# Expert gates of tokens 128 to 255 by scattered writes in HBM, those of tokens 0 to 127 by one-hots laid out per token

## The chip, the cores and the metric

The kernel runs on one core of a Trainium2 chip. The metric is the time of one execution on the device, from the first to the last instruction, in microseconds (us); a kernel's time is the median of its timed runs. The engines are TensorE (PE in the rows, PEld for its weight loads), VectorE (DVE), ScalarE (ACT), GpSimd (POOL) and SyncE (SP), each of which works through its own instruction stream in order and waits for others by semaphores.

## The reference

x is [1, 256, 1024] f32. Two transformer blocks run one after the other. The first has mixed attention and retention and a gated FFN (w_gate, w_up, w_down); the second has a gated mixing and a banded attention, and then the part that the change touches: a layer of 16,384 experts of which each token uses 8 heads times 16.

```python
def block(xb):                                    # 128 tokens, twice
    q = (xb @ w_query).reshape(128, 8, 2, 128)
    sc = einsum('thpd,hpkd->thpk', q, sub_keys)   # 128 keys in each half
    s_top, i_top = top_k(sc, 16)
    cand = s_top[:, :, 0, :, None] + s_top[:, :, 1, None, :]
    cand_idx = i_top[:, :, 0, :, None] * 128 + i_top[:, :, 1, None, :]
    best, pos = top_k(cand, 16)                   # of the 256 sums
    eidx = take_along_axis(cand_idx, pos)         # the expert: a * 128 + b
    g = softmax(best)
    h = gelu(einsum('thkd,td->thk', expert_u[eidx], xb))
    return einsum('thk,thkd->td', g * h, expert_v[eidx])
```

## The kernel before

The experts are not gathered. `peer` (L702) computes the hidden value of all 16,384 experts for all 256 tokens, and multiplies it by a matrix of gates that is zero wherever a token did not choose an expert. S, [128, 128, 256] f32, holds it: the first index of an expert, a, on the partitions, the second, b (called j), in the middle, and the token last.

Every f32 weight is taken in two parts. `unit_` (L80) loads 128x1024 f32 (`raw`, L89, on SyncE's DMA queue), ACT rounds it to `whi` (L94) and DVE subtracts to get `wlo` (L95). `mm3` (L105) then makes three matmuls, lines L107, L108 and L109.

The stages that matter here, in order of time:

- The first block's FFN: 22 steps f, each with a unit of w_gate and one of w_up.
- Queries and selection. `query(c)` makes the 16 halves of the queries and their scores. `choose` (L729) finds the top 16 of each head with DVE's MAX8 instructions, and when all eight heads are done, `decode` (L745) turns the positions into a, b and the softmax gate. These steps form a list, and `pump` takes a budget of them at a time between the matmul groups (PQ and PU), so that DVE's work lies beside PE's.
- First layer, `first_layer(j)` for j = 0 to 127: 24 matmuls of 256 columns from a unit of `peer_u`, then the gelu for every pair of j (L933 for tokens that already have their gate in S, with DVE's multiply L934; L936 for the others).
- Combine. From the point at which the decode is done, `combine` (L851) makes the gate matrix for four tokens at a time, beside the first layer. A one-hot row of a, A, and a one-hot row of b times the gate, G (two f16 parts, so that the gate keeps its precision), are multiplied on PE, summed over the 128 choices: 8 matmuls of 128 columns (L872), and DVE and ACT put the result into S (L875, L878). 64 combines make 512 such matmuls. They stand in pairs, in runs of 16 between the first layer's matmuls. A and G are laid out [128, 128, 4], with the four tokens innermost, so the 128 columns of one token lie four elements apart:

```python
nc.tensor.matmul(C[:, t * 128:t * 128 + 128], lhsT=A[:, :, t], rhs=G[i][:, :, t], start=i == 0, stop=i == 1)
```

- Second layer, for j = 0 to 127: S[:, j] is split in two parts (`split`, ACT L151 and DVE L152, tiles `keys` and `q`), and 12 matmuls of 512 columns (L974) multiply it by a unit of `peer_v`. The residual x3, parked in HBM, is loaded again behind j = 32 (L991), added at the end, and the result stored.

The program is ordered by a scheduler that follows the order of the code, except that `unit_` runs at a higher priority, so that loads and conversions of weights stand well ahead of their use.

Of the kernel before, what the change touches and what calls it, by code (L numbers as in the profile page):

```python
# [7 lines left out]
F32 = mybir.dt.float32  # L8
# [14 lines left out]
GP = 115  # L23
# [5 lines left out]
T = 256  # L29
D = 1024  # L30
# [5 lines left out]
for _n, _w in (("norm_mix", 8), ("norm_ffn", 8), ("final_norm", 8), ("ln_mix", 8), ("ln_ffn", 8),  # L36
               ("ret_gain", 8), ("gmlp_gain", 4), ("q_g", 1), ("k_g", 1), ("sinks", 8)):
    SMALL[_n] = (_o, _o + _w)
    _o += _w
# [3 lines left out]
class Net:  # L43
# [36 lines left out]
    def unit_(self, src, n, pieces, engine, between):  # L80
# [11 lines left out]
        for i in range(pieces):  # L92
            s = slice(i * n // pieces, (i + 1) * n // pieces)
            self.last_copy = nc.scalar.activation(hi[:, s], raw[:, s], AF.Copy).ins  # L94
            (engine or nc.vector).tensor_tensor(out=lo[:, s], in0=raw[:, s], in1=hi[:, s].bitcast(F32),  # L95
                                                op=OP.subtract)
# [17 lines left out]
    def gemm_t(self, ps, src, hl, K, k0=0, first=True, last=True, parts=None, engine=None):  # L114
        """ps[n, t] += W[k, n] x[k, t] for one unit of up to 8 k."""
# [12 lines left out]
    def gemm_t_late(self, jobs, hl):  # L128
        """gemm_t of several (ps, src), with the last k after all others."""
# [6 lines left out]
    def gemm_n(self, src, hl):  # L136
        """two banks, one per 128 tokens, of [t, 512] for a chunk of 512 columns."""
# [19 lines left out]
    def rsqrt(self, y, ss, n, scale, pool=None):  # L157
        """y = (ss * scale + eps)^-1/2, all [128, n]."""
# [22 lines left out]
    def token_sums(self, acc):  # L181
        """[128 t, 2] from [128 d, 256 t] summed over d."""
# [6 lines left out]
    def rows(self, r, name):  # L189
        """[128, 256] with r of token t in column t, in every partition."""  # L190
# [40 lines left out]
    def block1(self, actp):  # L231
        nc, a, tc = self.nc, self.a, self.tc
        mult, add, sub = OP.mult, OP.add, OP.subtract
        with ExitStack():
# [16 lines left out]
            self.iota16 = self.const.tile([128, 128, 4], F16, name="iota16")  # L251
            nc.sync.dma_start(out=self.iota16, in_=a["iota16"])
# [107 lines left out]
            with ExitStack() as s1:  # L360
                p = self.pool("ffn", 1, s1)
                p2 = self.pool("ffn2", 2, s1)
                hid = self.new_acts(p, KF, "hid", 1)
                early = []
                for f in range(KF):
# [336 lines left out]
    def peer(self, st, x3, h, acc):  # L702
        nc, a, tc = self.nc, self.a, self.tc
        mult, add, sub = OP.mult, OP.add, OP.subtract
        with tc.using_default_side("right"):
            xb = self.new_acts(self.pool("xb", 1), tag="xb", bufs=1)
            gs = self.pool("gs", 1).tile([128, 4, T], F16, name="gs")
            qp = self.pool("query", 1)
            late = ExitStack()
            p = self.pool("topk", 1, late)  # L710
        hand = self.pool("hand", 2, st)
        x3t = tc.dram_tile([2, 128, D], F32, name="x3t")
        stop = p.tile([128, 8, 2, 2, 16], F32, name="stop")
        itop = p.tile([128, 8, 2, 2, 16], U32, name="itop")
        best = p.tile([128, 8, 2, 16], F32, name="best")
        pos = p.tile([128, 8, 2, 16], U32, name="pos")
# [12 lines left out]
        def choose(hd):  # L729
            sc = scores.pop(hd)  # L730
            yield from top16([(sc[:, tb, e], stop[:, hd, tb, e], itop[:, hd, tb, e])
                              for tb in range(2) for e in range(2)], 205)
            cand = p.tile([128, 2, 80], F32, name="cand", bufs=2)
            s1, s2 = stop[:, hd, :, 0], stop[:, hd, :, 1]
# [10 lines left out]
        def decode():  # L745
            e16 = p.tile([128, 2, 16, 8], F16, tag="cand", name="e16", bufs=2)
            t8 = p.tile([128, 8, 2, 16], U32, tag="sc", name="t8", bufs=SC)
            dec = p.tile([128, 4, 2, 16, 8], F16, tag="stop", name="dec")
            a16, b16 = dec[:, 0], dec[:, 1]

            def spot(x):
                return x.rearrange("p t k h -> p h t k")

            for e in range(2):
                yield 340, lambda: nc.vector.tensor_copy(spot(dec[:, 2 + e]), itop[:, :, :, e])
            yield 340, lambda: nc.vector.tensor_scalar(t8, pos, 56, None, op0=add)
            yield 340, lambda: nc.vector.tensor_scalar(spot(e16), pos, 72.0, 0.0, op0=sub, op1=OP.max)
            yield 340, lambda: nc.vector.tensor_scalar(t8, t8, 3, None, op0=OP.logical_shift_right)
            yield 340, lambda: nc.vector.tensor_scalar(spot(a16), t8, 8.0, 0.0, op0=sub, op1=OP.max)
            yield 340, lambda: nc.vector.tensor_scalar(t8, pos, 16.0, 8.0, op0=OP.is_lt, op1=mult)  # L760
            yield 340, lambda: nc.vector.scalar_tensor_tensor(spot(b16), spot(a16), -8.0, pos, op0=mult, op1=add)
            yield 340, lambda: nc.vector.scalar_tensor_tensor(spot(b16), t8, -8.0, spot(b16), op0=add, op1=add)
            yield 200, lambda: nc.vector.tensor_tensor(out=a16, in0=a16, in1=e16, op=add)
            yield 200, lambda: nc.vector.tensor_tensor(out=b16, in0=b16, in1=e16, op=sub)
            ex = p.tile([128, 8, 2, 16], F32, tag="itop", name="ex")
            yield 340, lambda: nc.vector.tensor_tensor(out=ex, in0=best,
                                                       in1=best[:, :, :, 0:1].to_broadcast([128, 8, 2, 16]), op=sub)
            yield 10, lambda: nc.scalar.activation(ex, ex, AF.Exp)
            sm = p.tile([128, 8, 2], F32, name="sm")
            yield 340, lambda: nc.vector.tensor_reduce(out=sm, in_=ex, axis=AX.X, op=add)  # L770
            yield 200, lambda: nc.vector.reciprocal(sm, sm)
            yield 340, lambda: nc.vector.tensor_tensor(out=best, in0=ex,
                                                       in1=sm[:, :, :, None].to_broadcast([128, 8, 2, 16]), op=mult)
            for tb in range(2):
                pick = p.tile([128, 3, 128], F32, tag="sc", name="pick", bufs=SC)
                for e, x in ((0, a16), (1, b16)):
                    for k in range(0, 16, 8):
                        oh = p.tile([128, 16, 64], F16, tag="sc", name="oh", bufs=SC)
                        o4 = oh.rearrange("p a (k h) -> p a k h", h=8)
                        x4 = x[:, tb, k:k + 8].rearrange("p k h -> p (k h)").rearrange("p (r q) -> p r q", q=4)  # L780
                        yield 600, lambda: nc.vector.tensor_tensor(
                            out=oh.rearrange("p a (r q) -> p a r q", q=4),
                            in0=self.iota16[:, 0:16, None, :].to_broadcast([128, 16, 16, 4]),
                            in1=x4[:, None].to_broadcast([128, 16, 16, 4]), op=OP.is_equal)
                        yield 600, lambda: nc.vector.tensor_tensor(
                            out=o4, in0=o4, in1=dec[:, 2 + e, tb, :, None, :].to_broadcast([128, 16, 8, 8]), op=mult)
                        for n in (8, 4, 2):
                            yield 60 + 33 * n, lambda: nc.vector.tensor_tensor(
                                out=oh[:, 0:n], in0=oh[:, 0:n], in1=oh[:, n:2 * n], op=add)
                        yield 100, lambda: nc.vector.tensor_tensor(out=pick[:, e, k * 8:k * 8 + 64], in0=oh[:, 0],  # L790
# [295 lines left out]
```

## Time and profile before

| | us |
|---|---|
| median of 3 timed runs (1341.74 to 1342.67) | 1341.83 |
| span of the profiled execution | 1343.6 |
| PE busy in it | 1334.3 |
| DVE busy | 935.0 |
| ACT busy | 768.4 |
| GpSimd busy | 9.7 |

The mean granted clock of TensorE over the span is 0.997 of full speed. A timeline row of the trace gives a start in us from the span's start, a duration, the engine, the line of the program, and the tiles; "x16" means that so many instructions are drawn together, and a bracket at its end gives the time for which the engine sat idle ahead of it and what released it. Ends of matmuls are modelled: the distance between starts is what tells PE's pace.

### The profile page before, as it was taken

What the parts mean: (1) busy time and instruction counts of PE and PEld (TensorE: products, weight loads), DVE (VectorE), ACT (ScalarE), POOL (GpSimd) and SP (SyncE); (2) the same over time, 40 slices, a digit from 0 to 9 for tenths busy, and PEclk for the clock granted to TensorE, in tenths of its full rate; (3) what the DMA queues carried; (4) which work ended last, traced back from release to release, by engine and by line L of the source; (5) the groups of instructions that cost most, each with busy time, mean ns of one, the idle gap of its engine ahead of it and who ended that gap; (6) DMA issues with size and microseconds to landing.
All of it is one profiled execution on the core that took longest, in us unless ns stands there. A gap on an engine that the chain in (4) does not pass through costs nothing.

```text
span 1343.6 us, 24086 instructions
## 1 busy us (share of the span) xinstructions
PE 1334.3 (99%) x9384; PEld 1245.0 (93%) x9384; DVE 935.0 (70%) x1826; ACT 768.4 (57%) x1306; POOL 9.7 (1%) x12
## 2 busy tenths in 40 slices
PE   8999999999999999999999999999999999999998
PEld 8878999999998899999999999999998888888887
DVE  6767576766666977966996667777656666665665
ACT  5456445544455766444458887776555555555553
POOL 2000000000000000000000000000000000000000
PEclk8999999999999999999999999999999999999999
DMA  8545666666566446656564444444576666666664
GB/s 267 179 137 159 187 179 185 186 189 181 176 192 228 142 138 181 191 180 184 151 197 147 142 141 137 140 137 139 157 219 190 192 198 191 194 195 191 196 194 126
DMA packets 67633, 236.27 MB, mean 176 GB/s; under 512 B 7616, under 2 KB 9536, under 8 KB 67392
## 3 DMA queue, kind: packets, MB, share of 16 engines
q1 hardware_dynamic: 66512, 233.14, 57.1%
q8 instruction: 73, 1.20, 0.4%
q10 hardware_dynamic: 1008, 1.61, 0.3%
q14 instruction: 40, 0.33, 0.1%
HBM read 232.62 MB, written 2.10 MB: 175 GB/s over the span
## 4 chain that ended last, share of the span: by engine, by line
PE 95%; DVE 2%; DMA 1%; issue 0%; ACT 0%; POOL 0%; SPq 0%; ACTq 0%; POOLq 0%; DVEq 0%
PE ax L974 26%; PE mm L107 21%; PE mm L109 21%; PE mm L108 21%; PE ax L872 5%; DVE wlo L95 1%; DMA raw<-in_w_in_a_dram 1%; PE ax L837 0%; DMA xT<-in_xT_dram 0%; ACT whi L94 0%; PE ax L663 0%; PE ax L698 0%; PE ax L464 0%; PE ax L452 0%; PE ax L685 0%
## 5 line engine op out<-in xcount | busy, mean ns | idle before, releaser
L95 DVE TENSOR_TENSOR wlo<-raw,whi 128x1024 fp32r<-128x1024 f32 (+2 forms) x433 | 524.5, 1213 | 225.9 <-ACT whi L94 224.8
L94 ACT ACTIVATE whi<-raw 128x1024 fp32r<-128x1024 f32 (+3 forms) x439 | 458.0, 1046 | 332.9 <-PE mm L108 249.0
L107 PE MATMUL mm<-xbh,whi 128*128 128x256 f32 x1104 | 316.2, 287 | 0.0
L109 PE MATMUL mm<-xbh,wlo 128*128 128x256 f32 x1104 | 312.4, 283 | 0.8 <-DVE wlo L95 0.7
L108 PE MATMUL mm<-xbl,whi 128*128 128x256 f32 x1104 | 312.1, 283 | 0.0
L107 PE MATMUL mm<-acth,whi 128*128 128x256 f32 x848 | 241.0, 284 | 1.7 <-ACT acth L248 1.0
L108 PE MATMUL mm<-actl,whi 128*128 128x256 f32 x848 | 239.7, 283 | 0.7 <-DVE actl L249 0.7
L109 PE MATMUL mm<-acth,wlo 128*128 128x256 f32 x848 | 239.6, 283 | 0.0
L109 PEld LDWEIGHTS mm<-xbh,wlo 128*128 128x128 f32 x1104 | 210.6, 191 | 1.3 <-DVE wlo L95 1.2
L107 PEld LDWEIGHTS mm<-xbh,whi 128*128 128x128 f32 x1104 | 211.2, 191 | 0.2
L108 PEld LDWEIGHTS mm<-xbl,whi 128*128 128x128 f32 x1104 | 210.8, 191 | 0.0
L107 PEld LDWEIGHTS mm<-acth,whi 128*128 128x128 f32 x848 | 161.3, 190 | 2.8 <-ACT acth L248 1.2
L108 PEld LDWEIGHTS mm<-actl,whi 128*128 128x128 f32 x848 | 161.2, 190 | 1.6 <-DVE actl L249 1.6
L109 PEld LDWEIGHTS mm<-acth,wlo 128*128 128x128 f32 x848 | 161.3, 190 | 0.2 <-DVE wlo L95 0.2
L974 PE MATMUL ax<-wlo,keys 128*128 128x512 f32 x512 | 158.0, 389 | 0.0
L974 PE MATMUL ax<-whi,q 128*128 128x512 f32 x512 | 158.0, 389 | 0.0
L974 PE MATMUL ax<-whi,keys 128*128 128x512 f32 x512 | 157.9, 389 | 0.0
L151 ACT ACTIVATE keys<-S 128x256 fp32r<-128x256 f32 x128 | 53.4, 418 | 151.5 <-PE ax L974 151.5
L974 PEld LDWEIGHTS ax<-whi,q 128*128 128x128 f32 x512 | 96.1, 188 | 20.0
L974 PEld LDWEIGHTS ax<-wlo,keys 128*128 128x128 f32 x512 | 96.1, 188 | 19.9
L974 PEld LDWEIGHTS ax<-whi,keys 128*128 128x128 f32 x512 | 96.1, 188 | 19.8
L865 ACT ACTIVATE G<-B,ga 128x128 f16<-128x128 f16 x256 | 98.0, 575 | 0.0
(277 smaller groups left out, 1468.7 us busy)
## 6 DMA issues: line engine op xcount, KB each, us to landing
raw<-in_peer_u_dram SPq DMA_DIRECT2D x128, 512.0 KB, 3.6
raw<-in_peer_v_dram SPq DMA_DIRECT2D x128, 512.0 KB, 4.2
raw<-in_w_in_b_dram SPq DMA_DIRECT2D x32, 512.0 KB, 4.3
raw<-in_w_in_a_dram SPq DMA_DIRECT2D x31, 512.0 KB, 3.9
raw<-in_w_gate_dram SPq DMA_DIRECT2D x22, 512.0 KB, 3.6
raw<-in_w_up_dram SPq DMA_DIRECT2D x22, 512.0 KB, 3.7
raw<-in_w_out_dram SPq DMA_DIRECT2D x16, 512.0 KB, 4.3
raw<-in_w_down_dram SPq DMA_DIRECT2D x16, 512.0 KB, 3.6
```

What stands on the lines that cost most here:

```text
L94: self.last_copy = nc.scalar.activation(hi[:, s], raw[:, s], AF.Copy).ins
L95: (engine or nc.vector).tensor_tensor(out=lo[:, s], in0=raw[:, s], in1=hi[:, s].bitcast(F32), op=OP.subtract)
L107: mm(ps, lhsT=left[0], rhs=right[0], start=first, stop=False)
L108: mm(ps, lhsT=left[0], rhs=right[1], start=False, stop=False)
L109: mm(ps, lhsT=left[1], rhs=right[0], start=False, stop=last)
L151: nc.scalar.activation(hi, src, AF.Copy)
L865: nc.scalar.activation(G[0][:, :, t], B[:, :, t], AF.Copy, scale=ga[:, t0 + t:t0 + t + 1])
L872: nc.tensor.matmul(C[:, t * 128:t * 128 + 128], lhsT=A[:, :, t], rhs=G[i][:, :, t], start=i == 0, stop=i == 1)
L974: nc.tensor.matmul(banks[tb][d], lhsT=s[left][:, ts], rhs=w[right][:, d * 512:d * 512 + 512], start=first, stop=end)
```

## The change

Tokens 0 to 127 keep the combine, with other layouts: A and G are now [128, 4, 128], the columns of one token side by side, and 32 combines make 256 matmuls (L940). One group's one-hots are formed ahead of the group that PE multiplies.

Tokens 128 to 255 get their gates through HBM. `cmat` is an HBM tile of 128x128x128 f32, 8.4 MB, filled with zeros by 16 DMAs of 512 KB on SyncE's queue during the first block's FFN. The decode runs once for every two heads. Behind each of the four, 32 indirect DMAs on GpSimd's queue add one gate for each of the 128 tokens into `cmat`; those of a head follow those of the head before. Behind the first layer, 32 DMAs on GpSimd's queue load 256 KB of `cmat` each (tile `C`, three buffers), and DVE multiplies them into S for tokens 128 to 255, two of them ahead of the second layer and the others eight steps of j ahead. The gelu of a pair is two halves (L1001 with the multiply L1002 for tokens that have their gate, L1004 for the others). The reload of x3 moves from behind j = 32 to behind j = 120.

The diff, cut to its core:

```diff
+                zero = p.tile([128, 1024], F32, name="zero")
+                nc.gpsimd.memset(zero, 0.0)
+                self.cmat = tc.dram_tile([128 * 128 * TH, 1], F32, name="cmat")
...
+                    if 5 <= f < 21:
+                        self.blanked.append(nc.sync.dma_start(out=blank[:, (f - 5) * 1024:(f - 4) * 1024],
+                                                              in_=zero).ins)
...
-        def decode():
+        def decode(h0):
...
+            def put():
+                for hd in range(2):
+                    own = []
+                    for k in range(16):
+                        i = nc.gpsimd.indirect_dma_start(
+                            self.cmat, bass.IndirectOffsetOnAxis(ap=ps[:, hd, 1, k:k + 1], axis=0),
+                            bs[:, hd, 1, k:k + 1], None, compute_op=add).ins
...
+                        for o in put_by:
+                            tc.add_manual_dep(i, o.name, after, reason="heads add to the same places")
+                        own.append(i)
+                    put_by[:] = own
...
         def all_steps():
             for hd in range(8):
...
                 yield from choose(hd)
-            yield from decode()
+                if hd % 2:
+                    yield from decode(hd - 1)
+            yield from turn_picks()
...
+            A = cp.tile([128, 4, 128], F16, name="A", bufs=2)
+            B = cp.tile([128, 4, 128], F16, name="B")
+            G = [cp.tile([128, 4, 128], F16, name=f"G{i}", bufs=2) for i in range(2)]
...
-            A = cp.tile([128, 128, 4], F16, name="A", bufs=2)
-            B = cp.tile([128, 128, 4], F16, name="B", bufs=2)
-            G = [cp.tile([128, 128, 4], F16, name=f"G{i}", bufs=2) for i in range(2)]
...
-                    nc.tensor.matmul(C[:, t * 128:t * 128 + 128], lhsT=A[:, :, t], rhs=G[i][:, :, t], start=i == 0,
+                    nc.tensor.matmul(C[:, t * 128:t * 128 + 128], lhsT=A[:, t], rhs=G[i][:, t], start=i == 0,
                                      stop=i == 1)
...
+        groups.close()
+        with tc.using_default_side("right"):
+            gp = self.pool("gates", 1, groups)
+        cview = self.cmat.rearrange("(a b t) o -> a b (t o)", a=128, b=128)
+
+        def gates(j):
+
+            C = gp.tile([128, 4, 128], F32, name="C", bufs=3)
+            i = nc.gpsimd.dma_start(out=C, in_=cview[:, j:j + 4]).ins
+            for o in put_by:
+                tc.add_manual_dep(i, o.name, after, reason="all heads have been added")
+            with tc.issue_after(self.last_low):
+                nc.vector.tensor_tensor(out=S[:, j:j + 4, TH:], in0=S[:, j:j + 4, TH:], in1=C, op=mult)
+
+        gates(0)
+        gates(4)
...
-            if j == 32:
+            if j % 4 == 0 and j < 120:
+                gates(j + 8)
+            if j == 120:
                 groups.close()
```

Three places in the order of the instructions. In the rows a tile's number tells its copies apart.

DVE where the first layer gives way to the second, before: the last three combines and gate multiplies, weight splits, and the two lines L152 that make the lo parts of S for j = 0 and 1 (L934 at the end is the first layer's last gate multiply).

```order
L875 SCALAR_TENSOR_TENSOR S_6217<-ax_12050,S_6217 128x116x4
L95 TENSOR_TENSOR wlo_12158<-raw_12156,whi_12157 128x1024
L152 TENSOR_TENSOR q_12456<-S_6217,keys_12455 128x256
L152 TENSOR_TENSOR q_12478<-S_6217,keys_12477 128x256
L95 TENSOR_TENSOR wlo_12192<-raw_12190,whi_12191 128x1024
L934 TENSOR_TENSOR S_6217<-S_6217,gt_12122 128x512
```

The same place on DVE after.

```order
L96 TENSOR_TENSOR wlo_12041<-raw_12039,whi_12040 128x1024
L1002 TENSOR_TENSOR S_6240<-S_6240,gt_11974 128x2x128
L1047 TENSOR_TENSOR S_6240<-S_6240,C_11982 128x4x128
L1047 TENSOR_TENSOR S_6240<-S_6240,C_11985 128x4x128
L155 TENSOR_TENSOR q_11999<-S_6240,keys_11998 128x256
L1047 TENSOR_TENSOR S_6240<-S_6240,C_12014 128x4x128
L155 TENSOR_TENSOR q_12024<-S_6240,keys_12023 128x256
```

The split of S for j = 0 stood ahead of the first layer's last gate multiply and now stands behind it, with two multiplies by loaded gates (L1047) in between.

ACT at the same place, before (L151 makes the hi parts of S for j = 0 and 1, L933 is the first layer's last gelu).

```order
L878 ACTIVATE S_6217<-ax_12050 128x12x4
L151 ACTIVATE keys_12455<-S_6217 128x256
L151 ACTIVATE keys_12477<-S_6217 128x256
L94 ACTIVATE whi_12191<-raw_12190 128x1024
L933 ACTIVATE gt_12122<-mm_12061 128x512
```

And after.

```order
L95 ACTIVATE whi_12040<-raw_12039 128x1024
L1001 ACTIVATE gt_11974<-mm_11913 128x256
L1004 ACTIVATE S_6240<-mm_11913 128x2x128
L154 ACTIVATE keys_11998<-S_6240 128x256
L154 ACTIVATE keys_12023<-S_6240 128x256
```

Here too the hi parts of S (L154, formerly L151) moved from ahead of the last gelu to behind it.

SyncE's queue in the first block's FFN, after: the zeros (L389) stand between the loads of the weights, which alone stood there before.

```order
L389 DMA cmat_2480<-zero_2476 128x1024
L90 DMA raw_2489<-in_w_up_dram 128x1024
L389 DMA cmat_2480<-zero_2476 128x1024 x2
L90 DMA raw_2563<-in_w_gate_dram 128x1024
L389 DMA cmat_2480<-zero_2476 128x1024
L90 DMA raw_2593<-in_w_up_dram 128x1024
```

One to three writes moved in ahead of a load at a time; no load changed its place among the loads.

## Rows read from the trace of the kernel before

**Rows 1.** The page: span, busy time of each engine, chain that ended last.

```profile
span 1343.6 us, 24086 instructions
PE 1334.3 (99%) x9384; PEld 1245.0 (93%) x9384; DVE 935.0 (70%) x1826; ACT 768.4 (57%) x1306; POOL 9.7 (1%) x12
PE 95%; DVE 2%; DMA 1%; issue 0%; ACT 0%; POOL 0%; SPq 0%; ACTq 0%; POOLq 0%; DVEq 0%
```

**Rows 2.** Windows: stretch, us, busy PE, PEld, DVE, ACT, POOL, PEclk, DMA share, GB/s.

```profile
9.20:16.10 6.90, 6.73 (x31) 6.14 (x30) 6.69 (x16) 4.54 (x12) 1.61 (x2) 0.51 0.93 334
198.00:246.00 48.00, 48.00 (x408) 48.00 (x407) 35.45 (x67) 27.25 (x43) 0.00 (x0) 1.00 0.63 187
540.00:560.00 20.00, 20.00 (x169) 20.00 (x169) 19.97 (x100) 9.02 (x11) 0.00 (x0) 1.00 0.54 163
712.00:957.00 245.00, 245.00 (x2052) 242.80 (x2052) 176.32 (x342) 186.62 (x440) 0.00 (x0) 1.00 0.47 139
991.00:1339.00 348.00, 348.00 (x1538) 288.30 (x1538) 209.92 (x256) 186.94 (x253) 0.00 (x0) 1.00 0.63 190
```

**Rows 3.** Timeline of PE: a run of combine matmuls among the first layer's.

```profile
803.75 2.05 PE L872 MATMUL ax<-G,A 128*128 128x128 f16 x16
805.55 0.37 PE L107 MATMUL mm<-xbh,whi 128*128 128x256 f32 x1
805.75 0.28 PE L108 MATMUL mm<-xbl,whi 128*128 128x256 f32 x1
805.87 0.28 PE L109 MATMUL mm<-xbh,wlo 128*128 128x256 f32 x1
```

**Rows 4.** Instructions of line 872: durations (ns, min/median/max), first and last start.

```profile
L872 PEld LDWEIGHTS <-A x512: 110/117/136, 711.9 to 956.5; 128*128 128x128 f16 x171
L872 PE MATMUL ax<-G,A x512: 283/297/304, 711.9 to 956.6; 128*128 128x128 f16 x171
```

**Rows 5.** Timeline of all engines where the second layer begins.

```profile
991.17 0.28 PE L109 MATMUL mm<-xbh,wlo 128*128 128x256 f32 x1
991.29 0.63 PE L974 MATMUL ax<-whi,keys 128*128 128x512 f32 x2
991.37 1.06 ACT L94 ACTIVATE whi<-raw 128x1024 fp32r<-128x1024 f32 x1 [1.82 <-PE mm L108]
...
992.33 0.58 ACT L933 ACTIVATE gt<-mm 128x512 f32<-128x512 f32 x1
992.46 1.23 DVE L95 TENSOR_TENSOR wlo<-raw,whi 128x1024 fp32r<-128x1024 f32 x1 [1.65 <-ACT whi L94]
...
993.61 0.68 DVE L934 TENSOR_TENSOR S<-S,gt 128x512 f32<-128x512 f32 x1
993.78 0.42 ACT L151 ACTIVATE keys<-S 128x256 fp32r<-128x256 f32 x1 [0.87 <-PE ax L974]
```

**Rows 6.** DMA issues of 256 KB: queue, count, KB each, median us to landing.

```profile
x3t<-xt ACTq DMA_DIRECT2D x4, 256.0 KB, 3.3
bs<-in_bs_dram SPq DMA_DIRECT2D x1, 256.0 KB, 5.5
out_dram<-x SPq DMA_DIRECT2D x2, 256.0 KB, 2.1
```

**Rows 7.** Groups of DVE instructions by shape: busy us, mean ns; and one of them.

```profile
L179 DVE TENSOR_TENSOR acc<-acc,sq 128x256 f32<-128x256 f32 x28 | 11.7, 418 | 0.2
L735 DVE TENSOR_TENSOR cand<-stop 128x32 f32<-128x32 f32 x2 | 0.3, 170 | 0.0
L761 DVE SCALAR_TENSOR_TENSOR dec<-dec,pos x1: 1336/1336/1336, 666.2 to 666.2; 128x256 f16<-128x256 f16 x1
```

**Rows 8.** Timeline of PE in the decode: its one wait for a weight split.

```profile
670.57 0.39 PE L109 MATMUL mm<-xbh,wlo 128*128 128x256 f32 x1 [0.66 <-DVE wlo L95]
```

**Rows 9.** Waits: who waits for whom, us in total, times, longest.

```profile
ACT whi L94 <- PE mm L108: 249.0, 171, 3.6
```

**Rows 10.** Timeline of DVE: two weight splits of the selection.

```profile
553.39 1.21 DVE L95 TENSOR_TENSOR wlo<-raw,whi 128x1024 fp32r<-128x1024 f32 x1
681.16 1.22 DVE L95 TENSOR_TENSOR wlo<-raw,whi 128x1024 fp32r<-128x1024 f32 x1
```

**Rows 11.** Instructions of line 89: issue of a load, ns, first and last start.

```profile
L89 SPq DMA_DIRECT2D raw<-in_peer_u_dram x128: 327/328/467, 506.8 to 973.6; - x128
```

More of the change, by code (lines that the diff above doesn't have):

```diff
@@ L29 @@
 T = 256
+TH = 128
 D = 1024
@@ L250, in block1 @@
             self.ident = self.load_const(self.const, "ident", [128, 128])
-            self.iota16 = self.const.tile([128, 128, 4], F16, name="iota16")
-            nc.sync.dma_start(out=self.iota16, in_=a["iota16"])
+            both = self.const.tile([128, 192], F16, name="iota16")
+            nc.sync.dma_start(out=both, in_=a["iota16"])
+            self.iota = both[:, :128]
+            self.iota16 = both[:, 128:].rearrange("p (a q) -> p a q", q=4)
             with ExitStack() as s1:
@@ new lines, in turn_picks @@
+        def turn_picks():
+            ps = self.ax_bank()
+            for i in range(3):
+                nc.tensor.transpose(ps[:, i * 128:i * 128 + 128], pick[:, i], self.ident)
+            g = ps[:, 256:384]
+            nc.scalar.activation(gs[:, 2:4], ps[:, :256].rearrange("p (i t) -> p i t", i=2), AF.Copy)
+            nc.scalar.activation(gs[:, 0], g, AF.Copy, scale=GSCALE)
+            yield 200, lambda: nc.vector.scalar_tensor_tensor(gs[:, 1], g, GSCALE, gs[:, 0], op0=mult, op1=sub)
@@ L849, in peer, with form, four, each @@
         S, cp, ga = None, None, None
+        made = 0
+        spread, formed = None, []
+        def form():
+            nonlocal made, spread
+            t0 = made
+            if t0 % 64 == 0:
+                spread = cp.tile([128, 3, 64, 4], F16, name="spread", bufs=2)
+                nc.scalar.activation(spread, gs[:, 1:4, t0:t0 + 64, None].to_broadcast([128, 3, 64, 4]), AF.Copy)
+            A = cp.tile([128, 4, 128], F16, name="A", bufs=2)
+            B = cp.tile([128, 4, 128], F16, name="B")
+            G = [cp.tile([128, 4, 128], F16, name=f"G{i}", bufs=2) for i in range(2)]
+            def four(x):
+                return x.rearrange("p t (r q) -> p t r q", q=4)
+            def each(i):
+                return spread[:, i - 1, t0 % 64:t0 % 64 + 4, None, :].to_broadcast([128, 4, 32, 4])
+            numbers = self.iota.rearrange("p (r q) -> p r q", q=4)[:, None].to_broadcast([128, 4, 32, 4])
+            nc.vector.tensor_tensor(out=four(B), in0=numbers, in1=each(3), op=OP.is_equal)
+            for t in range(4):
+                nc.scalar.activation(G[0][:, t], B[:, t], AF.Copy, scale=ga[:, t0 + t:t0 + t + 1])
+            nc.vector.tensor_tensor(out=four(A), in0=numbers, in1=each(2), op=OP.is_equal)
+            nc.vector.tensor_tensor(out=four(G[1]), in0=four(B), in1=each(1), op=mult)
+            formed.append((A, G))
+            made += 4
@@ L861, in combine @@
-            nc.vector.tensor_tensor(out=B, in0=self.iota16, in1=spread(3), op=OP.is_equal)
-            for i in range(2):
-                if i == 0:
-                    for t in range(4):
-                        nc.scalar.activation(G[0][:, :, t], B[:, :, t], AF.Copy, scale=ga[:, t0 + t:t0 + t + 1])
-                else:
-                    nc.vector.tensor_tensor(out=G[i], in0=B, in1=spread(i), op=mult)
-            nc.vector.tensor_tensor(out=A, in0=self.iota16, in1=spread(2), op=OP.is_equal)
+            A, G = formed.pop(0)
@@ L959, in peer @@
                         cp = self.pool("comb", 1, groups)
-                    ga = cp.tile([128, T], F32, name="ga")
+                    ga = cp.tile([128, TH], F32, name="ga")
                     nc.scalar.activation(ga, gs[:, 0], AF.Copy)
             elif j % 2:
-                while done < T and done * (GP - start) < T * (j - start):
+                while done < TH and (done + len(formed) * 4) * (GP - start) < TH * (j - start):
                     combine(j + 1)
-        while done < T:
+        while done < TH:
             combine(128)
+        groups.close()
[11 more added lines that the diff above has]
+        gates(4)
         banks = [[self.ax_bank() for _ in range(2)] for _ in range(2)]
```

146 lines of the change are left out of this document (79 added, 67 removed).

## The prediction

> **What bounds the kernel now.** Read the page first [rows 1]: TensorE (PE) is busy 99% of a span of 1343.6 us, and the chain of work that ended last is 95% PE. So the kernel ends when PE has run through its matmuls, and an edit counts in two ways only: by what it takes off PE's stream, and by the holes that it tears into it. The windows [rows 2] say where other engines could tear such holes: PE is busy for the whole of 198 to 246 us (the first block's FFN), of 712 to 957 (the combines among the first layer) and of 991 to 1339 (the second layer), at a granted clock of 1.00, which is 2.4 GHz; between 540 and 560 us, in the selection of experts, VectorE (DVE) is busy 19.97 of 20 us and is nearly the bound itself.
>
> Then the combines. In the timeline [rows 3] a run of 16 of their matmuls starts at 803.75 and the next f32 matmul at 805.55; the one after that follows 0.20 us later, not 0.12 as the next, so a run costs 1.80 + 0.08 = 1.88 us, 0.118 us a matmul. Read over the whole stage: the first and the last combine start at 711.9 and 956.5 [rows 4], the first layer ends at 991.29 [rows 5], and 1824 f32 matmuls at 0.12 us lie between, 218.9 us of 279.4; 60.5 us are left for 512 matmuls, again 0.118.
>
> What is a 128-column matmul's own time? The same engine takes 0.12 us for 256 columns at full clock, so 128 columns stream in about 0.06. The combine's matmul is paced at twice that, and its weight load takes 117 ns [rows 4], the pace itself. I read from it that the load of A, or the reading of G, sets the pace, both of which lie 4 elements apart here, and not the streaming.
>
> **The change: the combine's matmuls.** Half of them go: 256 x 0.118 = 30.2 us off PE. The other 256 get A and G as contiguous rows. No row shows a contiguous f16 load, so I bound it: 0.118 each if the layout does nothing; 0.053 if only streaming is left. That end is worked out from two paces: the second layer's 1538 matmuls of 512 columns in 348 us [rows 2] are 0.226 each, 0.107 more than 0.12 for 256 columns more, so 128 columns are 0.053. I take 0.07, near the streaming end, since the f32 loads hide wholly behind 0.12 us of streaming and a load without the stride should do so here nearly: 256 x 0.07 = 17.9 us (13.6 to 30.2). PE's stream gets 60.5 - 17.9 = **42.6 us** shorter; at the old pace 30.3. Building the one-hots stays hidden: half as many groups, on engines that are busy 176 and 187 of 245 us there [rows 2].
>
> **The hand-over to the second layer.** Here the change adds a wait. Before, DVE and ScalarE (ACT) split S for j = 0 and 1 some eight instructions ahead of the first layer's end, so PE goes from its last L109 at 991.17 to L974 at 991.29 without a gap [rows 5]. After, tokens 128 to 255 of S need a gate that is loaded: the tile C stands in memory which the last gelu tile, read by the last L1002 multiply, still holds, so its GpSimd DMA waits for that multiply, DVE's L1047 waits for the DMA, ACT's L154 for L1047, and PE's first second-layer matmul for L154. Nothing else is left for PE. Queued on DVE behind the waiting L1047 are the second L1047, the lo splits and the weight splits. Step by step, from PE's last first-layer matmul at 991.17: the last gate multiply begins at 993.61 today, 2.44 us later (the gelu waits behind a 1.06 us weight conversion on ACT, then the multiply behind a 1.23 us one on DVE); it takes 0.42 at half width, as the 128x256 row in [rows 7]; the 256 KB load lands after 3.3 (bounds 2.1 and 5.5, other 256 KB transfers [rows 6]; no row shows one on GpSimd's queue); L1047 takes 0.68, as the 128x512 multiply at 993.61; L154 0.42, as L151 at 993.78. Less the 0.12 between matmuls: 7.1 us, 5.9 to 9.3. The second L1047 stands ahead of the lo split: +0.5 (0.2 to 1.2). PE idles throughout, and after the idle opening of the kernel the granted clock was 0.51, the 1.2 GHz level, for 6.9 us [rows 2], which lost 3.4; so 0 to 3.4 here, and I take 2. Sum: **+9.6 us** (6 to 14).
>
> **The selection.** The wide decode (one operation of 128x256 takes 1336 ns; a small one of 128x32 takes 170 [rows 7]) becomes four narrow ones. Some 17 operations at 0.2 us or a little over, four times, for 15 at 0.3 to 1.3: DVE gets about 5 to 9 us more work, while ACT and PE keep theirs. The cover is thin: with today's wide operations PE waits once, 0.66 us for a DVE weight split [rows 8]. Without those operations that stall may go (-0.7); with DVE full it may come more often (+3). I take 0.
>
> **The zeros.** 16 writes of 512 KB join SyncE's queue between the loads of w_gate and w_up, 8.4 MB in a stretch of 48 us where DMA is already busy 0.63 [rows 2]. At 187 GB/s for 0.63, they would fill the rest to nearly 1.0 of the stretch. The loads queued behind them slip by up to 8 to 10 us. What hides it: the weight conversions on ACT wait for PE to free buffers, 249 us in all [rows 9], not for loads, which land in 3.6 us and stand ready a long way ahead. 0, and +12 if that cover fails.
>
> **Scatters, gate loads, x3.** 128 scatters stand on GpSimd's queue, which has nothing else to do there. In DVE's order the first two heads' decode now ends behind the weight split that runs at 553.39 today, the last two's behind the one at 681.16 [rows 10]; those are the scatters' starts. They must be done at about 951 (the 993.6 of the hand-over less 42.6). That is 398 us for 128, 3.1 each, since each head waits for the one before: no cost, if an average scatter takes less. The 32 gate loads come 8 steps ahead, DVE gets 32 x 0.68 = 22 us more beside 210 busy of 348 [rows 2]: 0. x3, moved behind j = 120, is issued some 19 us ahead of its use and takes less than that: 0.
>
> **Sum.** -42.6 + 9.6 = -33.0 us. The profiled span of 1343.6 is 1.8 us above the timed median of 1341.83; the difference is made on the span and taken off the median: 1341.8 - 33.0 = **1309**.
>
> **The rivals.**
> (B) *The contiguous load is no faster.* Then half the matmuls go at their old pace: -30.3 + 9.6 = -20.7, **1321**. For it: the f16 load of 117 ns is a full 128x128 load, and no row tells its stride's part. Against: f32 loads of as many columns are hidden behind 0.12 us together with their matmul. I give 20%. The Trainium skill ("TensorE: Matmul & The Clock Gate", "Weight-path perf modes — Fast Weight Load (FWL) and DoubleRow") says that a fast load comes on for any load of 128 columns that isn't FP32, whether columns lie packed or with a stride. By that rule A loads fast already and rows bring nothing, which is this rival; the 117 ns of rows 4 speak against a fast load today, since the same page's slow load of 128 columns would be an estimated 107 ns.
> (C) *Backlog.* DVE, full in the selection, or the loads behind the zeros starve PE for about 12 us more (10 of the zeros' slip, some 2 of stalls): **1321**. For: 19.97 of 20 us. Against: 249 us of waiting on PE as slack. 13%.
> (D) *The scatters come late: slower.* A scatter is 128 elements of 4 bytes, each added in memory. If one takes more than 3.1 us on average, the first gate load waits, and PE with it: each 0.1 us above costs 12.8 us, so from about 3.37 us each (33 us late) the kernel is slower than before; at 4 us it is 115 us late, **1423**. The bounds are 0.33 us (today's issue of a load on SyncE's queue [rows 11], if only issuing counts) and 5.5 (if each waits for a landing such as the slowest in rows 6). Up to 8 of a head may be in flight, which puts it nearer the low end: 7%. The Trainium skill ("SBUF — State Buffer", "A bandwidth-pool intuition that's wrong (but worth ruling out)") gives about 620 ns for a DMA issued by GpSimd alone and about 3100 beside certain VectorE copies. No row here shows such a DMA; its high figure gives an estimate of 397 of the 398 us, just in time.
> (E) *It does less than it says,* gain and stall cancel: 3%, about **1340**.
>
> **How the numbers follow.** The forecast of **1309** has 57%; B 20, C 13, D 7, E 3. Its own range is 1300 (stall 6 us, load hidden: 1341.8 - 46.8 + 6, rounded) to 1314. The stated range reaches to B and C with a stall of up to 14 us: 1300 to 1326. Left out are D, E and about 8 in 100 of tails. Faster by over 0.2% (2.7 us, about what a measurement of this kernel can tell from no change): 0.90. Within 0.2%: 0.02. Slower: 0.08, D and a point of E.
>
> **What would show it.** Right: runs of 8 combine matmuls in about 0.6 us instead of 0.95; a single PE hole of 6 to 12 us where L109 gives way to L1058, ended by ACT L154, and on DVE L1047 waiting for C. Wrong: combine matmuls still 0.118 apart (B); PE waits for DVE L96 between 540 and 720 us, or for loads between 198 and 260 (C); the first C landing long after the last L1002, its DMA waiting on the scatters' queue (D).

## The result

| | median us | runs |
|---|---|---|
| before | 1342.05 | 1341.74 to 1342.67, 4 runs |
| after | 1307.07 | 1306.75 to 1307.48, 4 runs |

The ratio is 0.9731, with a 95% interval of 0.9718 to 0.9745: 35.0 us faster. Forecast were 1309 us and a range of 1300 to 1326.

### The profile page after: what moved, and what is told of

Read it like the earlier page. It is cut to its first block, busy times and chain, and to the rows that moved or that the text cites. A ratio compares the mean times of both kernels' runs of the same rounds, so it can differ in the third digit from the quotient of the medians.

```text
span 1305.5 us, 23587 instructions
## 1 busy us (share of the span) xinstructions
PE 1285.2 (98%) x9125; PEld 1196.0 (92%) x9125; DVE 906.7 (69%) x1790; ACT 719.9 (55%) x1163; POOL 262.9 (20%) x173
## 4 chain that ended last, share of the span: by engine, by line
PE 97%; DVE 2%; DMA 1%; issue 0%; ACT 0%; ACTq 0%; DVEq 0%
PE ax L1058 27%; PE mm L110 22%; PE mm L111 22%; PE mm L112 22%; PE ax L940 1%; PE ax L886 1%; DVE wlo L96 0%; DMA C<-cmat 0%; DMA small<-in_small_dram 0%; ACT whi L95 0%; PE ax L676 0%; PE ax L711 0%; PE ax L477 0%; PE ax L465 0%; PE ax L698 0%
## 5 line engine op out<-in xcount | busy, mean ns | idle before, releaser
L830 POOL DMA_INDIRECT cmat<-best,pos x128 | 235.1, 1837 | 215.9 <-DVE itop L739 153.7
L112 PE MATMUL mm<-acth,wlo 128*128 128x256 f32 x848 | 236.3, 279 | 0.0
L154 ACT ACTIVATE keys<-S 128x256 fp32r<-128x256 f32 x128 | 53.4, 418 | 161.4 <-PE ax L1058 155.4
```

The source lines that it names most:

```text
L112: mm(ps, lhsT=left[1], rhs=right[0], start=False, stop=last)
L154: nc.scalar.activation(hi, src, AF.Copy)
L830: i = nc.gpsimd.indirect_dma_start(self.cmat, bass.IndirectOffsetOnAxis(ap=ps[:, hd, 1, k:k + 1], axis=0), bs[:, hd, 1, k:k + 1], None, co ...
```

## The profile after

The page of the changed kernel, as [rows 1] of before. TensorE (PE) makes 259 matmuls fewer and is still busy 98% of the time; GpSimd (POOL), which had 9.7 us, now has 262.9.

```profile
span 1305.5 us, 23587 instructions
PE 1285.2 (98%) x9125; PEld 1196.0 (92%) x9125; DVE 906.7 (69%) x1790; ACT 719.9 (55%) x1163; POOL 262.9 (20%) x173
PE 97%; DVE 2%; DMA 1%; issue 0%; ACT 0%; ACTq 0%; DVEq 0%
```

A run of combine matmuls in the timeline of PE after, to be held against [rows 3]: 8 matmuls start at 788.10 and the next f32 matmul at 788.53, the one behind it 0.20 later.

```profile
788.10 0.62 PE L940 MATMUL ax<-G,A 128*128 128x128 f16 x8
788.53 0.36 PE L110 MATMUL mm<-xbh,whi 128*128 128x256 f32 x1
788.73 0.28 PE L111 MATMUL mm<-xbl,whi 128*128 128x256 f32 x1
```

So a run of 8 costs 0.43 + 0.08 = 0.51 us, 0.064 a matmul, where it was 0.118. Within the run the pace is 0.43 / 8 = 0.054, where it was 1.80 / 16 = 0.1125. All 32 runs cost 16.4 us (the sum of their starts to the next matmul, with the extra 0.08 us each); before, 60.7.

The hand-over to the second layer, timeline of all engines after; [rows 5] is the same place before.

```profile
941.98 0.28 PE L112 MATMUL mm<-xbh,wlo 128*128 128x256 f32 x1
942.18 1.06 ACT L95 ACTIVATE whi<-raw 128x1024 fp32r<-128x1024 f32 x1 [1.82 <-PE mm L111]
943.14 0.36 ACT L1001 ACTIVATE gt<-mm 128x256 f32<-128x256 f32 x1
943.27 1.22 DVE L96 TENSOR_TENSOR wlo<-raw,whi 128x1024 fp32r<-128x1024 f32 x1 [1.65 <-ACT whi L95]
...
944.41 0.42 DVE L1002 TENSOR_TENSOR S<-S,gt 128x256 f32<-128x256 f32 x1
945.13 1.71 POOL L1043 DMA_DIRECT2D C<-cmat  x3 [80.12 <-DVE S L1002]
949.05 0.69 DVE L1047 TENSOR_TENSOR S<-S,C 128x512 f32<-128x512 f32 x1 [4.22 <-DMA C<-cmat]
949.77 0.72 ACT L154 ACTIVATE keys<-S 128x256 fp32r<-128x256 f32 x2 [5.99 <-DVE S L1047]
...
950.16 0.69 DVE L1047 TENSOR_TENSOR S<-S,C 128x512 f32<-128x512 f32 x1 [0.42 <-DMA C<-cmat]
...
950.24 1.22 PE L1058 MATMUL ax<-whi,keys 128*128 128x512 f32 x2 [7.98 <-ACT keys L154]
```

Read from the bottom: PE waited 7.98 us for the hi part of S (L154), that for the gate multiply (L1047), that 4.22 us for the landing of C, and GpSimd, which issues C's DMA and had been idle for 80 us, for the last L1002. TensorE's windows (stretch, us, busy PE, PEld, DVE, ACT, POOL, PEclk, DMA share, GB/s) show the granted clock: the first row's 0.75 is the mean over a fall from 1.00 to 0.50 within the hole, and it stays at 0.50, the 1.2 GHz level, until 956.

```profile
942.00:950.00 8.00, 0.26 (x3) 0.06 (x1) 2.25 (x3) 1.83 (x4) 1.71 (x3) 0.75 0.69 230
954.00:956.00 2.00, 2.00 (x7) 1.52 (x6) 0.43 (x1) 0.65 (x2) 0.00 (x0) 0.50 0.25 96
957.00:960.00 3.00, 3.00 (x14) 2.45 (x14) 1.56 (x3) 1.48 (x2) 0.00 (x0) 1.00 0.32 79
```

From 941.98 to the 240th matmul of the second layer, 11.1 us are lost against the steady paces: 8.1 in the hole, 3.0 at the lower clock. Before, the same sum is 0.03.

## The experiments

### One part alone: the layout, for all 256 tokens

`rows_all` is the kernel before with the one-hots per token, formed one group ahead as in the changed kernel, and nothing in HBM. The layout lines of its edit:

```diff
-            A = cp.tile([128, 128, 4], F16, name="A", bufs=2)
+            A = cp.tile([128, 4, 128], F16, name="A", bufs=2)
...
-                    nc.tensor.matmul(C[:, t * 128:t * 128 + 128], lhsT=A[:, :, t], rhs=G[i][:, :, t], start=i == 0,
+                    nc.tensor.matmul(C[:, t * 128:t * 128 + 128], lhsT=A[:, t], rhs=G[i][:, t], start=i == 0,
```

> The kernel before with one part of the change alone: the one-hots of all 256 tokens laid out per token, 512 combine matmuls, no gates through HBM. If the layout sets the pace, a run of 16 takes 16 x 0.064 = 1.03 us instead of 1.89 and the kernel gains 512 x (0.1185 - 0.064) = 27.9 us: about 1314 us, and the second layer begins without a gap. If the rows bring nothing by themselves (the Trainium skill's rule in the page TensorE: Matmul & The Clock Gate, section Weight-path perf modes, by which strided columns load as fast as packed ones), the pace stays 0.118 and the time 1342 us.

Measured: 1312.04 us, a ratio to before of 0.9771 (0.9755 to 0.9788), 30.0 us faster. In the timeline of PE a run of 16 starts at 802.99 and ends 0.87 later.

```profile
802.99 1.07 PE L893 MATMUL ax<-G,A 128*128 128x128 f16 x16
803.86 0.36 PE L107 MATMUL mm<-xbh,whi 128*128 128x256 f32 x1
804.07 0.28 PE L108 MATMUL mm<-xbl,whi 128*128 128x256 f32 x1
```

That is 0.054 again, and 0.060 with the 0.08 that a run costs, shared by 16 instead of 8: 30.9 us for 512 matmuls, 29.8 less than before. This part alone is worth 30.0 us of the change's 35.0. That it is the layout, and not the forming ahead, the next runs show.

### Which side sets the pace

Three kernels made from the changed one take the old layout back for A, for G, and for both; all three keep the forming ahead. The edit for G (`rearrange` gives the old storage the new order of indices):

```diff
-            G = [cp.tile([128, 4, 128], F16, name=f"G{i}", bufs=2) for i in range(2)]
+            G = [cp.tile([128, 128, 4], F16, name=f"G{i}", bufs=2).rearrange("p b t -> p t b") for i in range(2)]
```

> The changed kernel with A and G laid out four elements apart again, as before the change; 128 tokens still by combine, 128 through HBM. If the layout sets the pace: 0.118 a matmul, 256 x 0.054 = 13.9 us more than the changed kernel, about 1321 us (the rival B of the prediction). If shorter runs or earlier one-hots made the matmuls faster: 0.064 still, 1307 us.

> The changed kernel with only A, the side that is loaded as weights, four elements apart. If the weight load sets the pace: 0.118 a matmul and about 1321 us, as with both. If the reading of G does: 0.064 and 1307 us. If each is a limit of its own, something between for one of the two.

> The changed kernel with only G, the side that streams, four elements apart. If the weight load sets the pace: 0.064 a matmul and 1307 us. If the reading of G does: 0.118 and about 1321 us.

| four elements apart | us | all 32 runs, us | per matmul |
|---|---|---|---|
| neither (the changed kernel) | 1307.07 | 16.4 | 0.064 |
| A (loaded as weights) | 1306.77 | 17.0 | 0.066 |
| G (streamed) | 1322.02 | 29.6 | 0.116 |
| both | 1320.2 | 30.4 | 0.119 |

Each of the three variants ran once; the last two columns are read from its trace. PE waits for nothing within these runs of matmuls, so the building of the one-hots doesn't set their pace. The stride of G nearly doubles the time of a matmul and that of A hardly costs anything. The instructions' own durations don't say so; here line 940 of `a_strided` and then of `g_strided` (ns, min/median/max, first and last start).

```profile
L940 PEld LDWEIGHTS <-A x256: 112/113/137, 707.2 to 914.0; 128*128 128x128 f16 x128
L940 PE MATMUL ax<-G,A x256: 219/219/248, 707.2 to 914.0; 128*128 128x128 f16 x128
```

```profile
L940 PEld LDWEIGHTS <-A x256: 96/115/118, 708.8 to 928.1; 128*128 128x128 f16 x128
L940 PE MATMUL ax<-G,A x256: 274/294/296, 708.8 to 928.2; 128*128 128x128 f16 x128
```

The weight load takes 113 ns in the one and 115 in the other, while the matmuls of a run follow each other every 56 ns in the one (0.45 us for 8) and every 105 in the other (0.84), as the timelines of `a_strided` and then of `g_strided` show.

```profile
788.40 0.64 PE L940 MATMUL ax<-G,A 128*128 128x128 f16 x8
788.85 0.36 PE L110 MATMUL mm<-xbh,whi 128*128 128x256 f32 x1
```

```profile
788.04 1.08 PE L940 MATMUL ax<-G,A 128*128 128x128 f16 x8
788.88 0.37 PE L110 MATMUL mm<-xbh,whi 128*128 128x256 f32 x1
```

A load that takes 113 ns and keeps a pace of 56 overlaps its neighbours; its duration is no pace.

That matmuls keep their pace with a strided load of A, 0.056 us for 0.054, agrees with the Trainium skill ("TensorE: Matmul & The Clock Gate", "Weight-path perf modes — Fast Weight Load (FWL) and DoubleRow"), which has its fast load for columns packed or strided. For the streaming side the nearest page is "SBUF — State Buffer", section "Door 1: The DMA port swizzle (why `[64,N]` ≈ `[32,N]`)", by which reads run at full bandwidth as long as two of them fall into one line of 16 bytes. G had two f16 values in each 16 bytes and still streamed at half the pace; the measurement decides.

### The hole at the hand-over

`early_gates` loads the gates of j = 0 to 7 into memory that A and G gave up after the last combine at 913 us, multiplies them ahead of the first layer's end, and starts the others five steps of j ahead.

```diff
+        def early_gates():
+            for j in range(0, 8, 2):
+                C = cp.tile([128, 2, 128], F32, tag="A" if j < 4 else "G0", name="C0", bufs=2)
+                i = nc.gpsimd.dma_start(out=C, in_=cview[:, j:j + 2]).ins
...
+                if j == 123:
+                    early_gates()
...
-        gates(0)
-        gates(4)
...
-            if j % 4 == 0 and j < 120:
-                gates(j + 8)
+            if j % 4 == 3 and j < 120:
+                gates(j + 5)
```

> The changed kernel with the gates of j = 0 to 7 loaded into memory of the combine's tiles, which is free from about 913 us on, and multiplied into S ahead of the first layer's end; the other gate loads start four steps of j ahead or a little more. If the hole at the hand-over is the chain last gate multiply, gate load, L1047, L154, it goes with the clock's fall behind it: 11 us off, about 1296 us. If a later wait takes its place (the last gelu, or DVE waiting for the next gate load): 1300 to 1307 us.

Measured: 1297.04 us (1296.02 to 1297.96, 4 runs), a ratio to before of 0.9641 (0.9625 to 0.9657). `late_puts`, which is told below and turned out to run as the changed kernel does, took 1306.69 us on the same chip at a ratio of 0.9715 (0.9698 to 0.9731): 9.65 us more; its hole and its clock cost 10.3 in the profile. (The kernel before took 1344.97 us there, the median of 7 runs, so the change is worth 38.3 us on that chip and 35.0 on the other.) First PE's timeline at the hand-over, where 0.12 us lie between the last matmul of one layer and the first of the other; then the four early multiplies on DVE (ns, first and last start), done 16 us before.

```profile
943.64 0.28 PE L112 MATMUL mm<-xbh,wlo 128*128 128x256 f32 x1
943.76 0.63 PE L1068 MATMUL ax<-whi,keys 128*128 128x512 f32 x2
```

```profile
L938 DVE TENSOR_TENSOR S<-S,C x4: 418/418/421, 926.0 to 927.0; 128x256 f32<-128x256 f32 x4
```

The loss at the hand-over is 0.03 us, as before the change, and no later wait took its place. This version beats both kernels.

`fill_hole` leaves the hole and keeps TensorE busy in it.

```diff
+FILL = 64
...
+        idle = self.mm_bank()
+        for i in range(FILL):
+            nc.tensor.matmul(idle[:, :T], lhsT=xb[0][:, i % 8, :128], rhs=xb[0][:, i % 8], start=True, stop=True)
```

> The changed kernel with 64 idle f32 matmuls of 256 columns, 7.7 us, on TensorE behind the first layer's last matmul; their result is read by nobody. They lie in the hole of 8.2 us. If the granted clock fell because TensorE stood idle, it stays at 1.00 and the 2.9 us that the first matmuls of the second layer lost come back: 1304 us. If it fell for another reason: 1307 us.

Measured: 1305.61 us (1304.99 to 1306.37), 1.1 less than `late_puts` on the same chip. Its windows, beside those of the changed kernel above: the clock stays at 1.00.

```profile
942.00:950.00 8.00, 8.00 (x67) 7.82 (x66) 2.03 (x3) 1.60 (x3) 1.71 (x3) 1.00 0.72 226
954.00:956.00 2.00, 2.00 (x11) 1.65 (x10) 1.32 (x2) 0.89 (x1) 0.00 (x0) 1.00 0.30 109
```

Eleven matmuls fit into the two microseconds that held seven. The first matmuls of the second layer lose 0.2 us here; in eight profiles with an idle hole of 8 to 9 us they lose 1.6, 1.6, 1.7, 1.8, 1.9, 1.9, 2.6 and 3.0. So the clock's share was expected too high from one profile; that the idle hole brings it is shown.

### The scatters

```diff
-            yield 10, put
+            puts.append(put)
+            if h0 == 6:
+                for q in puts:
+                    yield 10, q
```

> The changed kernel with all 128 scatters issued behind the last two heads' decode, from about 680 us on, rather than in four parts from 568 us. In the changed kernel the 128 took 296 us to 863 us, 2.3 us each. If they keep that, they end at about 975 us, 30 us behind the first gate load's place at 945, and the kernel takes about 1338 us. If they are faster once the selection is over (1.55 us of issue each, as the fastest), they end at about 880 us and the time stays 1307 us.

`late_puts` moves the code that issues the scatters behind the last decode. It gives 1306.69 us (1306.53 to 1306.82), but it tells nothing of the question: with nothing else on GpSimd's queue its first scatter started at 567.9 us all the same, as soon as its own head was decoded. `late_start` makes, on top of this edit, the first scatter wait for the last heads' decode (`lasts` holds the last operation of each decode):

```diff
+                        if h0 == 0 and hd == 0:
+                            tc.add_manual_dep(i, lasts[-1].name, after, reason="start late")
```

> The changed kernel with the first scatter waiting for the last heads' decode, at about 678 us (listing the scatters behind it in the code alone had let them start at 568 us all the same). At the period of the changed kernel, 2.33 us a scatter, they end at about 981 us with the last one's landing, 36 us behind the point (945 us) at which the first gate load is issued: about 1343 us, and a hole of some 44 us. If scatters were paced by the selection's work on DVE and speed up behind it (1.55 us): done at 877 us, 1307 us.

Measured: 1336.86 us. Scatters from 675.2 to 971.9 us, 2.34 us apart on average, and a hole of 38.2 us at the hand-over (41.0 with the clock), 29.9 more than the changed kernel's 11.1. The rows of GpSimd in its timeline show what a scatter costs: while DVE works, in the hole, and with its wait for the head before.

```profile
934.38 2.58 POOL L831 DMA_INDIRECT cmat<-best,pos  x1 [0.30 <-issue]
937.26 2.57 POOL L831 DMA_INDIRECT cmat<-best,pos  x1 [0.30 <-issue]
943.10 2.49 POOL L831 DMA_INDIRECT cmat<-best,pos  x1 [3.27 <-DMA cmat<-best,pos]
945.90 1.55 POOL L831 DMA_INDIRECT cmat<-best,pos  x1 [0.31 <-issue]
947.76 1.55 POOL L831 DMA_INDIRECT cmat<-best,pos  x1 [0.30 <-issue]
...
971.91 1.55 POOL L831 DMA_INDIRECT cmat<-best,pos  x1 [0.30 <-issue]
975.55 1.72 POOL L1049 DMA_DIRECT2D C<-cmat  x3 [2.08 <-DMA cmat<-best,pos]
```

In the hole, with DVE idle, one follows the other every 1.86 us; while DVE works it is up to 2.89, and at a change of heads 4 to 6. DVE's rows of the same time show what lengthens one: a weight split that is already running when it starts.

```profile
937.19 1.23 DVE L96 TENSOR_TENSOR wlo<-raw,whi 128x1024 fp32r<-128x1024 f32 x1 [1.66 <-ACT whi L95]
942.95 1.22 DVE L96 TENSOR_TENSOR wlo<-raw,whi 128x1024 fp32r<-128x1024 f32 x1 [1.65 <-ACT whi L95]
```

The scatter of 937.26 ends 1.41 us after the first of them, that of 943.10 ends 1.42 after the second. In the changed kernel 50 of the 128 scatters start while a split runs, and all 50 end 1.42 to 1.56 us after it; the other 78 take 1.55 in the median and 2.0 at most, though DVE works beside most of them too.

The expected 44 us of hole were 6 too many: the scatters began at 675 and not at 678 us, the last one landed 3.6 us behind its issue and not 5, and those in the hole came faster. These 30 us are what the decode in four parts, and so the early start, is worth.

`no_puts` leaves the scatters out.

```diff
-            yield 10, put
```

> The changed kernel without the 128 scatters: the gates of tokens 128 to 255 stay zero, and their experts' part of the output is left out. If the scatters lie wholly beside other work: 1307 us, the same. If they cost DVE or the loads something that reaches TensorE: faster, by the 0.9 us that TensorE waits for DVE at 580 us or more.

Measured: 1305.93 us (1305.31 to 1306.18), 0.8 less than `late_puts` on the same chip: the scatters cost about that, and no more.

### The zeros

`zeros_twice` issues each write of zeros two times.

```diff
-                        self.blanked.append(nc.sync.dma_start(out=blank[:, (f - 5) * 1024:(f - 4) * 1024],
-                                                              in_=zero).ins)
+                        for _ in range(2):
+                            self.blanked.append(nc.sync.dma_start(out=blank[:, (f - 5) * 1024:(f - 4) * 1024],
+                                                                  in_=zero).ins)
```

> The changed kernel with each zero written twice: 32 writes of 512 KB among the loads. Once took the stretch to 0.91 of the DMA engines and 310 GB/s, with no wait on TensorE. Twice is 16.8 MB beside 9 MB of loads, at 330 GB/s some 78 us of transfers in 50: a slip of about 28 us for loads that are issued some 20 to 25 us ahead of their use. If that lead is all the cover there is: 3 to 10 us more, 1310 to 1317 us, with TensorE waiting for weight conversions between 200 and 260 us. If the slip is spread further: 1307 us.

Measured: 1307.7 us, the same. Its windows show the DMA engines at 0.94 for 94 us (0.63 before in the first stretch, [rows 2]; the changed kernel has 0.94 in the first and 0.71 in the second) and PE without a gap in them.

```profile
196.00:246.00 50.00, 50.00 (x430) 50.00 (x429) 37.69 (x70) 28.65 (x46) 0.96 (x1) 1.00 0.94 330
246.00:290.00 44.00, 44.00 (x376) 44.00 (x375) 30.34 (x39) 21.60 (x32) 0.00 (x0) 1.00 0.94 328
```

The slip was spread over twice the stretch, its last writes starting at 309 us, and never reached TensorE. 16.8 MB are hidden; how much more would be, no run shows.

### The 4 us that no step accounts for

Between the two profiles shown, 38.1 us of span went, 3 more than in the timed medians, and 4.1 of them lie ahead of 530 us, where the matmuls are the same.

> The kernel before, profiled once more. Its shown profile has f32 matmuls of 256 columns 0.1187 us apart between 130 and 420 us, where the changed kernel and every kernel made from it, with the same matmuls there, have 0.1167 and then 0.1178: 4 us by 530 us, which no step of the prediction accounts for. If that belongs to one execution, this profile shows 0.1167 and a span near 1340 us; if it belongs to the program, 0.1187 again and 1343 us.

> The changed kernel with its smaller table of numbers (192 f16 a partition) padded to the old size of 512, so that what is allocated behind it lies as before. If where the tiles lie in memory sets the pace of the early matmuls: 0.1187 us and about 4 us more, 1311 us. If not: 0.1167 and 1307 us.

The padding is one line:

```diff
-            both = self.const.tile([128, 192], F16, name="iota16")
+            both = self.const.tile([128, 512], F16, name="iota16")
```

The windows from 130 to 190 us (PE's matmuls in brackets) of before, of before once more, of after and of `after_padded`:

```profile
130.00:190.00 60.00, 60.00 (x508) 60.00 (x507) 39.40 (x58) 29.53 (x33) 0.00 (x0) 1.00 0.58 176
```

```profile
130.00:190.00 60.00, 60.00 (x514) 60.00 (x513) 39.84 (x59) 30.22 (x33) 0.00 (x0) 1.00 0.59 179
```

```profile
130.00:190.00 60.00, 60.00 (x516) 60.00 (x515) 40.16 (x60) 30.52 (x33) 0.00 (x0) 1.00 0.59 181
```

```profile
130.00:190.00 60.00, 60.00 (x508) 60.00 (x507) 39.24 (x57) 29.49 (x32) 0.00 (x0) 1.00 0.60 175
```

The same program, before, has 0.1187 us a matmul in one execution and 0.1173 in the other, with a span of 1339.8. So one program has both paces, and most of the 4 us lies between two executions of it: between this second profile of before and that of after lie 34.3 us. It isn't shown that the change has no part in them. `after_padded` was profiled at 0.1187, and its four runs (1308.28 to 1311.95, median 1309.58) all lie above those of the changed kernel. The eleven profiled kernels with the smaller table have 0.1167 in this window, and the three profiles with the larger one have 0.1187, 0.1173 and 0.1187. Whether the place of the tiles sets this pace, and so whether some of the 35.0 us is owed to the smaller table, stays open.

## Why the prediction was right, step by step

| term | predicted us | measured us | by |
|---|---|---|---|
| combine matmuls | -42.6 | -44.3 (60.7 to 16.4) | starts of all runs |
| hole at the hand-over | 7.6 | 8.1 | timeline after, `early_gates` |
| clock behind it | 2.0 | 3.0 (1.6 to 3.0 in eight profiles) | windows, `fill_hole` |
| selection, scatters | 0 | -0.6 | second profile of before against after |
| zeros, x3, gate loads | 0 | 0 | `zeros_twice`, no PE wait after |
| ahead of 530 us | none | -0.4 | the same two profiles |
| sum | -33.0 | -34.2 | spans 1339.8 and 1305.5: -34.3 |

**Combine.** The size was right within 1.7 us: within a run the matmuls reached the streaming end that the prediction had worked out, 0.054 to its 0.053; the value of 0.064 is that and 0.08 us for each run of 8, where 0.07 was taken. The reading under it was half wrong, and that the size came out all the same is in part luck. It named two candidates, the load of A and the reading of G, and then leaned on the first: that the load's 117 ns equalled the pace was taken as a sign against rival B. `a_strided` and `g_strided` show that the equality meant nothing. Rival B was wrong for another reason than the one given: the row layout brought next to nothing by the load (0.002 us a matmul), as its rule has it, and nearly all by the stream. Had the change laid out A alone per token, it would be `g_strided`: 1322 us, the time forecast for rival B.

**Hole.** Each link was there, in the order told. The last gate multiply began 2.43 us after PE's last matmul (2.44 forecast) and took 0.42. The landing was the mis-sized term: from the end of L1002 at 944.83 to L1047 at 949.05 are 4.2 us, 0.3 until GpSimd issues and 3.9 to the landing, for 3.3; it lies within the bounds of 2.1 and 5.5. The second L1047, for which 0.5 was added, cost nothing: it began at 950.16, 0.08 us ahead of PE's first matmul, and PE, which starts with the hi part and ran at half its clock, shows no further wait for the lo part.

**Clock.** The forecast took its price from the opening of the kernel [rows 2], where 6.9 us at 0.51 were said to have lost 3.4. The second profile of before has a clock of 1.00 in the same stretch:

```profile
9.20:16.10 6.90, 5.67 (x45) 5.25 (x44) 6.69 (x16) 4.54 (x12) 1.60 (x2) 1.00 0.95 330
```

DVE is busy 6.69 us of it in both, and by the 200th matmul the faster clock has won only 0.25 us (33.37 against 33.62). So the opening did not lose 3.4 us, and no row of before told how long the low clock would last behind the hole; that the measured 3.0 lies in the forecast's 0 to 3.4 is partly luck. Luck too is that two errors nearly cancel in the sum: the gain of the combine was forecast 1.7 us too small, the cost of hole and clock 1.5 too small.

**Selection.** The stall of [rows 8] is gone, as was held possible, and another came in its place, at the first pair's decode, where the timeline of PE after has the row below. Of the 0.6 us in the table, some 0.25 are three transposes on PE that the changed decode does without.

```profile
580.12 0.39 PE L112 MATMUL mm<-xbh,wlo 128*128 128x256 f32 x1 [0.94 <-DVE wlo L96]
```

**Scatters.** Rival D turned on 3.1 us each. They took 2.33 on average (567.7 to 863.5 us for 128), so some 80 us were left until the first gate load at 945.1. Of the forecast's remark that up to 8 of a head may be in flight, no run shows the number; from 3.1 to 6.4 us to the landing and 1.86 us or more between starts, an estimate is two to four. `late_start` shows the rival's mechanism at work when they begin 107 us later. No run shows the kernel slower than before for it.

**Rival C.** Neither the zeros nor DVE's backlog reached TensorE by more than the 0.94 us above. The 249 us that the forecast held against it are a sum over the whole program; between 190 and 262 us, where the zeros go, the weight conversions wait 21.1 us for PE. What shows that the cover holds is `zeros_twice`.

**What the change is worth.** `rows_all` has 30.0 of the 35.0 us without HBM. Halving the matmuls saves another 14.4 us on TensorE (30.85 to 16.42) and gives 11.1 back at the hand-over. That makes 33.3; the 1.7 left over no run accounts for. With the gates of j = 0 to 7 loaded early, and so without the hole, the change takes 1297 us.

## What to carry to other kernels

A duration that equals the pace does not say what sets the pace: undo the layout of one operand at a time. When work moves off the critical engine to a load, look for the first place at which that engine needs the loaded data, and see whether the load can start before it; here it waited for memory, not for data, and a load into memory that was free 30 us earlier took the hole away, 9.65 us of the kernel's time. An idle hole of 8 us cost more than its length here, since the clock fell in it.

## What the runs showed of the hardware

- f16 operands streamed into TensorE with a distance of four elements (8 bytes) run at about half the pace: 0.105 us for 128 columns within a run of 8 (0.1125 in runs of 16 with both operands strided), 0.054 packed. The same distance in the operand that is loaded as weights costs 0.002 us a matmul.
- A scatter of 128 single f32 values with addition, issued by GpSimd, takes 1.86 us from start to start when VectorE is idle, 1.55 of it on GpSimd, and up to 2.89 where a weight split of VectorE is running at its start: it then ends some 1.42 us after the split. In the prediction the Trainium skill ("SBUF — State Buffer", "A bandwidth-pool intuition that's wrong (but worth ruling out)") had 620 ns and 3100 ns for a DMA issued there; the runs have the ends closer together, 1.54 and 2.59 us on GpSimd, and the mean of 2.33 from start to start lies between the page's two.
- f32 matmuls of 256 columns had paces of 0.1187 and 0.1173 us in two executions of one program, both at a granted clock of 1.00; what sets the pace is not shown.
